# Quarter sums and weight sums on VectorE alone, a weight sum kept in DRAM, rope keys rotated in place, and query latents split earlier, in a one-core mixer kernel

## The chip, the cores and the metric

The kernel runs on one core of a Trainium2 chip. The metric is device time in microseconds of one execution. The kernel before was timed three times: 641.77, 641.38 and 640.35 us, with a median of 641.38 us. A profiled execution of it took 643.46 us, and the span from its first to its last instruction is 641.7 us.

## The reference

One inference step of a diffusion trunk with one layer: 128 prompt tokens and 1024 latent tokens (9 blocks of 128 rows), width 1024. Cut to what matters:

```python
h = rmsnorm(x) * (1 + scale) + shift              # scale, shift, gate from conditioning
u, v, g_a, c_q, c_kv, k_rope, g_b = split(h @ w_in)   # 512,512,512,256,128,64,512 columns
# group A: gated MLP over positions, 4 heads x 128, chunks of 128 positions
v = rmsnorm(gelu(v)) * g_v
a = gelu(u) * (einsum('hpq,bnqhd->bnphd', w_s, v) + b_s) * silu(g_a)
# group B: latent attention, 4 heads, low-rank queries and keys
q = rmsnorm(c_q) @ w_uq;  ckv = rmsnorm(c_kv);  k_rope = rope(k_rope)
attn = softmax(q_nope @ k_nope + rope(q_rope) @ k_rope) @ v     # latents also read 256 cached keys
y = x + gate * (concat(a, attn * silu(g_b)) @ w_o)
return rmsnorm(y) (prompt, latents), ckv, k_rope
```

## The kernel before, in words

**Numbers in two parts.** Every fp32 product is made of rounded parts: a value is rounded to a high part, the rest is a low part, and TensorE makes high x high, high x low and low x high. So each operand costs two evictions: a rounding ("high", on ScalarE or GpSimd) and a subtraction ("low", `lo_of`, L126, on VectorE alone).

**The seven products.** The columns u, g_a and g_b (1536, in three groups `q` = 0, 1, 2, each of two column blocks `j`) of the input projection are computed for the 1024 latent tokens by a scheme that needs seven products of half size where eight are usual. Their names are phases 1, 2, 5, 6, 3, 7, 4; "b" is a helper for the prompt. `SEQ` (L773) lists them in the order of work: 1 and 2 for all q, then 5 and 6, then "b" and 3, then 7 and 4. The matmuls are L868 (`pr`), 24 for one phase and column block in four groups of chunks, into a pool of six PSUM banks (`psa`). The prompt's products (L1006, `pps`) run between them and take a bank of a second pool of two (`pst`).

The activations come in four quarters A11, A12, A21, A22 (tiles `area00` to `area11`, high and low part of each). Phases 1, 2 and 4 read quarters as they are. Phases 5, 6, 7 and 3 read *quarter sums* s1, s2, s3, s4 (`sum_steps`, L957). For each half g of the rows: s1 is three additions (`s1a`, `s1b`, `s1c`), and s2, s3 and s4 are two each, from one another: s1 = A21 + A22, s2 = s1 - A11, s3 = A22 - s2, s4 = A12 - s2. One addition is a 128x1024 fp32 instruction (L968) on whichever of VectorE and GpSimd is to be done first. s1 lies in `mixB`, s2 and later s4 in `ss`, s3 in `st`. Each sum is then split (steps `ah`, `a`) over the quarter that it replaces as moving operand.

The weights come by DMA as raw tiles of 512 KB (`wr`, L786) on SP's queue. Phases 5, 6, 7 and 4 need *weight sums* (`weight_steps`, L792): `ws5` (L803), `ws6` (L812), `ws7` (L820), and for phase 4 two, `wt4` (L829) and `ws4` (L833). Then come the high part (`wh`) and the low part (`w`, L126) of the weights, in tiles `wop`. Raw tiles and `wop` pairs are few (`raw`: 2, later 3; `wop`: 2, later 3), so a load waits until an earlier raw tile is split.

**Around them.** Up to about 130 us the kernel modulates and transposes x and makes v and the gate: after GELU (L605) and statistics, `divide` (L619) scales v by its norm, most blocks on GpSimd, and TensorE mixes positions (L624, `mixp`), which VectorE takes out into `mixA` (L628). From 160 us the norms of the latents follow (`stat_steps`), which also multiply the key latents in place in `zraw`. Late in the products the query latents are transposed (`cq_steps`, L1157: transposes into a `pst` bank, high part on ScalarE, low part on VectorE), the query weights are folded (`fold_steps`, L1094, from four loads `fr`), and the rope keys are rotated (`ropek_steps`, L1285 to L1295: two products in tiles `ka` and `kb`, added twice into `kd`, on VectorE or GpSimd). The keys are transposed (L1318, `kT`) and the queries made (`qn`, `qr`, and their transposes L1236 with evictions L1268 and L1269), and then the scores begin (L1499). Attention takes from about 336 to 540 us and the output projection the rest; the change leaves both as they are.

**What sets the order.** All steps from the gate stage to the keys are given to class `Plan` (L43) with an engine ("V" VectorE, "G" GpSimd, "S" ScalarE, "T" TensorE, "D" SP's loads, "X" bookkeeping; "vG" and "SG" a choice of two), a cost, the steps that it depends on, a priority and resources that it takes and gives. `run` is a list scheduler: at each moment it emits the ready step with the smallest priority. A step on VectorE ("v") that overlaps one on GpSimd is charged a longer cost. The order in which steps are emitted is the order of each engine's instructions, and each engine works in that order.

Of the kernel before, what the change touches and what calls it, by code (L numbers as in the profile page):

```python
# [18 lines left out]
P = 128  # L19
# [23 lines left out]
class Plan:  # L43
# [8 lines left out]
    def run(self):  # L52
# [4 lines left out]
        while left:  # L57
# [4 lines left out]
            for s in left:  # L62
# [46 lines left out]
def tile_hymba_step(ctx: ExitStack, tc: tile.TileContext, I, O):  # L109
# [442 lines left out]
    VG2, COST2, HIGH2 = "vG", (1.25, 2.2), (1.05, 1.3)  # L552
# [45 lines left out]
    def post_steps(ts_):  # L598
# [176 lines left out]
    NEEDS = {1: ((0, 0),), 2: ((1, 0),), 5: ((0, 0), (0, 1)), 6: ((1, 1),), "b": ((0, 1),), 3: ((1, 1),), 7: ((1, 1), (0, 1)), 4: ((0, 0), (1, 0))}  # L775
# [6 lines left out]

    def raw_load(ph, q, y, c, prio):
        def fn():
            raws[ph, q, y, c] = place_for((ph, q, y, c), f"wr{ph}{q}{y}{c}", [2, 4, P])
            nc.sync.dma_start(raws[ph, q, y, c], I["w_t"][4 * q + c : 4 * q + c + 3 : 2, :, 4 * y : 4 * y + 4, :].rearrange("j p k m -> p j k m"))  # L786

        before = [order["load"] + "!"] if order["load"] else [f"wq{NK - 1}"]
        order["load"] = f"wr{ph}{q}{y}{c}"
        load_step(order["load"], fn, before, prio, 1.7, takes=("raw", "large"))  # L790

    def weight_steps(ph, q, prio):  # L792

        for y, c in NEEDS[ph]:
            raw_load(ph, q, y, c, prio)
        keys = [(ph, q, y, c) for y, c in NEEDS[ph]]
# [3 lines left out]
        if ph == 5:  # L800

            def total(e):
# [6 lines left out]
        elif ph == 6:  # L809

            def total(e):
# [4 lines left out]
            loaded = [f"ws6{q}"]  # L816
        elif ph == 7:

            def total(e):
# [5 lines left out]
            src, loaded, gone = (lambda: tsum[7, q]), [f"ws7{q}"], []  # L825
        elif ph == 4:

            def first(e):
                e.tensor_tensor(r(0), r(0), tsum[7, q], op=ALU.add)  # L829
                leave((7, q, 1, 1))  # L830

            def total(e):
# [3 lines left out]
            step(f"wt4{q}", VG2, COST2, first, [loaded[0], f"ws7{q}", f"w7{q}"], prio, gives=("raw", "large"))  # L836
            step(f"ws4{q}", VG2, COST2, total, [loaded[1], f"wt4{q}"], prio, gives=("raw", "large"))
# [434 lines left out]

    kd = {}

    def ropek_steps(t0, n):

        cell = {}

# [735 lines left out]
```

## Time and profile before

| | |
|---|---|
| median of three runs | 641.38 us |
| the profiled execution | 643.46 us |
| its span | 641.7 us |
| mean granted TensorE clock | 0.974 |
| TensorE busy | 612.9 us (96% of the span) |
| VectorE busy | 416.7 us (65%) |
| ScalarE busy | 286.2 us (45%) |
| GpSimd busy | 160.5 us (25%) |
| chain that ended last | PE 85%, DVE 6%, ACT 3%, issue 2%, DMA 1%, POOL 1% |

PE is TensorE's matmuls, PEld its weight loads, DVE VectorE, ACT ScalarE, POOL GpSimd, SP the engine that issues most DMAs. A row of the timeline gives start and length in us, engine, line, operation, the tile written, an arrow, and the tiles read, shapes, a count, and in brackets the idle time of the engine ahead of it with what ended it. A row of the groups gives busy time and mean ns of one. A row of the waits gives the total, how often, and the longest.

### The profile page before, as it was taken

How to read it: one execution, taken by the hardware profiler on the slowest of the kernel's cores; microseconds unless marked ns; L12 is line 12 of the kernel's file. 1: busy time of each engine (PE TensorE's matmuls, PEld its weight loads, DVE VectorE, ACT ScalarE, POOL GpSimd, SP SyncE). 2: the span in 40 equal slices, each digit the busy share in tenths (PEclk: the TensorE clock that was granted, in tenths of full speed). 3: DMA queues.
4: the chain of work that ended last, by engine and by line, in shares of the span. 5: the costliest groups of instructions: out<-in, count | busy, mean ns of one | idle time of the engine just before them, and what ended most of it. 6: DMA issues, size and time to landing. Idle time of an engine off the chain costs nothing.

```text
span 641.7 us, 9495 instructions
## 1 busy us (share of the span) xinstructions
PE 612.9 (96%) x3567; PEld 524.3 (82%) x3567; DVE 416.7 (65%) x838; ACT 286.2 (45%) x627; POOL 160.5 (25%) x145
## 2 busy tenths in 40 slices
PE   7799989999997999999789999999999999999995
PEld 6577877888885878888778899999999989888884
DVE  4435576714649875899685666577677666396655
ACT  4455864314242233444664555555555643232222
POOL 3523143102017220235352222123233241000001
PEclk8799989999999899999899999999999999999998
DMA  8970504401322424660100000000100112523211
GB/s 323 355 275 24 162 1 166 133 33 39 100 98 91 136 95 133 194 206 25 50 2 0 2 1 1 2 1 2 30 4 34 34 66 99 196 100 132 96 69 65
DMA packets 24509, 57.31 MB, mean 89 GB/s; under 512 B 2304, under 2 KB 6800, under 8 KB 24464
## 3 DMA queue, kind: packets, MB, share of 16 engines
q1 hardware_dynamic: 24320, 56.52, 25.7%
q8 instruction: 28, 0.46, 0.3%
q10 hardware_dynamic: 144, 0.20, 0.1%
q14 instruction: 17, 0.14, 0.1%
HBM read 51.88 MB, written 4.83 MB: 88 GB/s over the span
## 4 chain that ended last, share of the span: by engine, by line
PE 85%; DVE 6%; ACT 3%; issue 2%; DMA 1%; POOL 1%; SPq 0%; ACTq 0%; POOLq 0%
PE pr L868 16%; PE pT L1542 5%; PE w L1792 5%; PE w L1791 5%; PE w L1793 5%; PE s L1499 3%; PE o L1566 3%; PE o L1568 3%; PE o L1567 3%; PE s L1500 3%; PE s L1501 3%; PE s L1503 3%; PE s L1502 3%; PE vacc L402 3%; PE pps L1006 2%
## 5 line engine op out<-in xcount | busy, mean ns | idle before, releaser
L868 PE MATMUL pr<-area,wop 128*128 128x512 f32 x504 | 128.9, 398 | 4.7 <-DVE wop L126 2.9
L868 PEld LDWEIGHTS pr<-area,wop 128*128 128x128 f32 x504 | 91.7, 191 | 22.8 <-DVE wop L126 4.2
L126 DVE TENSOR_TENSOR pl<-pT,ph 128x512 fp32r<-128x512 f32 x81 | 55.4, 686 | 45.6 <-ACT ph L1546 45.3
L1490 POOL TENSOR_SCALAR e<-e,rs 128x1280 f32<-128x1280 f32 x32 | 42.8, 1338 | 138.7 <-DVE rs L1489 117.7
L1484 ACT ACTIVATE e<-s,nb,scl 128x256 f32<-128x256 f32 x64 | 56.1, 881 | 39.4 <-DVE nb L1478 33.3
L1546 ACT CAST ph<-pT 128x512 fp32r<-128x512 f32 x80 | 45.5, 590 | 40.0 <-PE pT L1542 37.2
L1791 PE MATMUL w<-area,areap 128*128 128x512 f32 (+1 forms) x152 | 57.8, 381 | 0.0
L1793 PE MATMUL w<-area,ml 128*128 128x512 f32 (+1 forms) x152 | 57.5, 378 | 0.0
L1792 PE MATMUL w<-area,areap 128*128 128x512 f32 (+1 forms) x152 | 57.5, 378 | 0.0
L1542 PE MATMUL pT<-ident,e 128*128 128x128 f32 x320 | 47.9, 273 | 0.7 <-DVE pl L126 0.7
L1566 PE MATMUL o<-ph,vh 128*128 128x256 f32 x160 | 48.1, 300 | 0.0
L1568 PE MATMUL o<-ph,vl 128*128 128x256 f32 x160 | 45.0, 281 | 0.0
L1567 PE MATMUL o<-pl,vh 128*128 128x256 f32 x160 | 44.9, 281 | 0.0
L1542 PEld LDWEIGHTS pT<-ident,e 128*128 128x128 f32 x320 | 37.8, 140 | 4.3 <-DVE pl L126 1.5
L1474 DVE TENSOR_REDUCE m<-s 128x1 f32<-128x1024 f32 x32 | 38.9, 1216 | 3.1 <-PE s L1503 3.1
L1499 PE MATMUL s<-kch,area 128*128 128x512 f32 (+1 forms) x96 | 38.5, 401 | 1.3 <-DVE areap L126 1.3
L126 DVE TENSOR_TENSOR wop<-wr,wop 128x1024 fp32r<-128x1024 f32 x21 | 32.6, 1553 | 9.9 <-ACT wop L557 6.3
L126 DVE TENSOR_TENSOR area<-hf,area 128x256 fp32r<-128x256 f32 (+3 forms) x25 | 17.2, 693 | 26.7 <-ACT hf L394 26.6
L1500 PE MATMUL s<-kcl,area 128*128 128x512 f32 (+1 forms) x96 | 34.6, 360 | 0.0
L1501 PE MATMUL s<-kch,area 128*128 128x512 f32 (+1 forms) x96 | 34.4, 359 | 0.0
L1503 PE MATMUL s<-krl,area 128*128 128x512 f32 (+1 forms) x96 | 34.3, 357 | 0.0
L1502 PE MATMUL s<-krh,area 128*128 128x512 f32 (+1 forms) x96 | 34.3, 357 | 0.0
(352 smaller groups left out, 1431.1 us busy)
## 6 DMA issues: line engine op xcount, KB each, us to landing
wr<-in_w_t SPq DMA_DIRECT2D x30, 512.0 KB, 3.7
ada<-in_ada_ss SPq DMA_DIRECT2D x16, 512.0 KB, 9.6
xr<-in_x SPq DMA_DIRECT2D x9, 512.0 KB, 3.9
adag<-in_ada_g SPq DMA_DIRECT2D x8, 512.0 KB, 3.3
wor<-in_w_o SPq DMA_DIRECT2D x8, 512.0 KB, 3.7
out_y<-y SPq DMA_DIRECT2D x8, 512.0 KB, 2.7
x<-in_x SPq DMA_DIRECT2D x6, 512.0 KB, 5.9
wvr<-in_w_v SPq DMA_DIRECT2D x8, 256.0 KB, 7.0
```

Source lines behind the costliest of these rows:

```text
L126: V.tensor_tensor(lo, src, f32(hi), op=ALU.subtract)
L868: T.matmul(ps, w[a][:, j % 2, k, :], x[:, k, b, :], start=first and ph in FIRST, stop=last, skip_group_check=ph not in FIRST)
L1484: S.activation(e[:, sl], src, AF.Exp, bias=nb, scale=scl[:, t : t + 1], accum_out=su[:, i : i + 1])
L1499: T.matmul(ps, qh_, kch[:, sl], start=True, stop=False)
L1500: T.matmul(ps, qh_, kcl[:, sl], start=False, stop=False)
L1542: T.transpose(ps[:, w : w + P], es[t, h][:, c * P : (c + 1) * P], ident)
L1566: T.matmul(o, vh[:, kt, :], ph[:, sl], start=c == 0, stop=False)
L1567: T.matmul(o, vh[:, kt, :], pl[:, sl], start=False, stop=False)
L1568: T.matmul(o, vl[:, kt, :], ph[:, sl], start=False, stop=c == n - 1)
L1791: T.matmul(ps, a, woh[k][:, c0:c1], start=k == 0, stop=False)
L1792: T.matmul(ps, a, wol[k][:, c0:c1], start=False, stop=False)
L1793: T.matmul(ps, b, woh[k][:, c0:c1], start=False, stop=k == NK - 1)
```

## The change

It does five things.

1. **One engine for the sums.** `VG2` becomes "v": all quarter sums and weight sums go to VectorE. The divides `gv` all go to VectorE too. The charge for an overlap of VectorE and GpSimd in `Plan.run` is computed from speeds of 0.36 and 0.67.
2. **A weight sum kept.** The sum `ws6` of phase 6 is also, up to rounding, the first sum of phase 4. A step `wt6` writes it to a DRAM tile `t2d` (three times 512 KB, on SP's queue), and phase 4 loads it (`wr4qt`) in place of the raw tile of weights that it took before; `wt4` is gone. The raw tile of phase 6 is given back only after the write has landed and phase 6's low part is made. The raw tile of phase 7 is given back after its low part.
3. **s4 in s1's place.** s4 is built in `mixB` where s1 was, and no longer in `ss`. So s3 waits only for `openB` (the end of the stage before) and s4 for the split of s1, and neither for the split of s2. For the last two column blocks `w5r` waits for the split of s4.
4. **Rope keys in place.** The rotation goes to VectorE, writes back into `zraw`, and reads tables of its own (`rk`, two more loads of 256 KB); it waits for its latents' statistics no longer, only for the projection. The doubling into `kd` becomes one copy on ScalarE.
5. **Query latents sooner.** The pool `zp` of the split query latents is opened in `open2` (when phases 6's and 7's sums are split and s4 is made) and not in `open3`; `cq` steps depend on `open2`.

The core of the diff:

```diff
@@ Plan.run
-                    r = min(self.shares[other] - now, 2 * cost)
-                    mine, theirs = (0.5 * r, 0.3 * r) if eng == "v" else (0.3 * r, 0.5 * r)
-                    cost += mine
+                    r = self.shares[other] - now
+                    slow, fast = (0.36, 0.67) if eng == "v" else (0.67, 0.36)
+                    if cost / slow <= r / fast:
+                        cost = cost / slow
+                        theirs = (1 - fast) * cost
+                    else:
+                        cost += (1 - slow) * r / fast
+                        theirs = r / fast - r
...
-    VG2, COST2, HIGH2 = "vG", (1.25, 2.2), (1.05, 1.3)
+    VG2, COST2, HIGH2 = "v", 1.25, (1.05, 1.3)
@@ post_steps
-            if j == 1 and n == 3:
-                step(f"gv{t}", "V", 0.72, lambda t=t, j=j: divide(j, t, V), [f"rv{t0}"], 0.5)
-            else:
-                step(f"gv{t}", "G", 1.1, lambda t=t, j=j: divide(j, t, G), [f"rv{t0}"], 1)
+            step(f"gv{t}", "v", 0.72, lambda t=t, j=j: divide(j, t, V), [f"rv{t0}"], 0.5)
@@ NEEDS, raw_load, weight_steps (NEEDS of phase 4: ((0, 0), (1, 0)) becomes ("t", (1, 0)))
+    t2d = gd.tile([3, P, 1024], F32, tag="t2d", name="t2d")
+            if y == "t":
+                raws[ph, q, y, c] = place_for((ph, q, y, c), f"wr{ph}{q}t", [2, 4, P])
+                nc.sync.dma_start(raws[ph, q, y, c], t2d[q].rearrange("p (j k m) -> p j k m", j=2, k=4))
+                return
...
-            loaded = [f"ws6{q}"]
+            loaded, gone = [f"ws6{q}"], []
+            step(f"wt6{q}", "D", 1.7, lambda: nc.sync.dma_start(t2d[q].rearrange("p (j k m) -> p j k m", j=2, k=4), r(0)), [f"ws6{q}"], prio - 0.5, lag=2.2)
+            step(f"wu6{q}", "X", 0.0, lambda: leave(keys[0]), [f"wt6{q}", f"w6{q}"], 0, gives=("raw", "large"))
...
-            def first(e):
-                e.tensor_tensor(r(0), r(0), tsum[7, q], op=ALU.add)
-                leave((7, q, 1, 1))
...
-            step(f"wt4{q}", VG2, COST2, first, [loaded[0], f"ws7{q}", f"w7{q}"], prio, gives=("raw", "large"))
-            step(f"ws4{q}", VG2, COST2, total, [loaded[1], f"wt4{q}"], prio, gives=("raw", "large"))
+            step(f"ws4{q}", VG2, COST2, total, loaded, prio, gives=("raw", "large"))
@@ sum_steps
-            sum_step(f"s3a{g}", lambda made=made: made(st, "st"), lambda q=q: q(A22, 0), lambda q=q: q(A22, 1), add, [f"a6.{g}"], 3.2)
+            sum_step(f"s3a{g}", lambda made=made: made(st, "st"), lambda q=q: q(A22, 0), lambda q=q: q(A22, 1), add, ["openB"], 3.2)
-            sum_step(f"s4a{g}", lambda here=here: here(ss), lambda q=q: q(A12, 0), lambda here=here: here(ss), sub, [f"a6.{g}", f"s3b{g}"], 3.1)
+            sum_step(f"s4a{g}", s1, lambda q=q: q(A12, 0), lambda here=here: here(ss), sub, [f"a5.{g}", f"s2b{g}"], 3.1)
@@ cq_steps, ropek_steps, open2
-        step(f"cp{t0}", "T", 0.22 * n, pe, ["open3"], 2.6 + 0.01 * t0, takes=("pst",))
+        step(f"cp{t0}", "T", 0.22 * n, pe, ["open2"], 2.6 + 0.01 * t0, takes=("pst",))
...
+            V.tensor_tensor(kr(0, 64), kr(0, 64), rk[0][:, ts_, :], op=ALU.mult)
+            V.tensor_tensor(kr(0, 64), kr(0, 64), cell["b"], op=ALU.add)
...
+            S.copy(kd[t0], kr(0, 64).unsqueeze(2).broadcast_to([P, n, 2, 64]))
...
-        step("open2", "X", 0.0, open2, [f"a{ph}.{g}" for ph in (7, 3) for g in range(2)], 0)
+        step("open2", "X", 0.0, open2, [*(f"a{ph}.{g}" for ph in (6, 7) for g in range(2)), "s4a0", "s4a1"], 0)
```

Lines of the changed kernel are 5 to 12 higher than before at these places (L968 becomes L975, L126 becomes L131, L619 becomes L624, L868 becomes L875).

GpSimd, at the first divides of the gate stage (L619, after whose `gv` TensorE mixes) and the first quarter sums (L968 into `mixB`), before:

```order
L129 TENSOR_SCALAR wq2_746<-wqr3_723 128x448
L619 TENSOR_TENSOR gv0_706<-gv0_706,vv3r_835 128x512
L619 TENSOR_TENSOR gv2_740<-gv2_740,vv3r_835 128x512
L968 TENSOR_TENSOR mixB_681<-mixB_681,area11_115 128x1024
L129 TENSOR_SCALAR wq4_997<-wqr4_730 128x448
L968 TENSOR_TENSOR mixB_681<-mixB_681,area11_115 128x1024
```

VectorE at the same place now (`areap` and `area11` are low parts of the transposed x):

```order
L131 TENSOR_TENSOR area11_115<-hf240_880,area11_115 128x256
L624 TENSOR_TENSOR gv0_707<-gv0_707,vv3r_835 128x512
L624 TENSOR_TENSOR gv1_714<-gv1_714,vv3r_835 128x512
L131 TENSOR_TENSOR areap_116<-hf241_902,areap_116 128x128
L624 TENSOR_TENSOR gv2_741<-gv2_741,vv3r_835 128x512
L131 TENSOR_TENSOR area11_115<-hf250_894,area11_115 128x256
L131 TENSOR_TENSOR areap_116<-hf251_918,areap_116 128x128
```

The divides have gone from GpSimd to VectorE, three within five instructions, and no quarter sum stands among them on either engine.

VectorE from the weight sum of phase 5 (`wr5001`, L803) on, where phases 2 and 5 meet; `wop122` is the low part of the weights for the last third of phase 2, `wop150` and `wop160` those for phases 5 and 6, before:

```order
L803 TENSOR_TENSOR wr5001_1754<-wr5001_1754,wr5000_1713 128x1024
L126 TENSOR_TENSOR wop122_1794<-wr2210_1637,wop022_1793 128x1024
L1027 TENSOR_TENSOR mixA_94<-mixA_94,poT10_1802 128x2x128
L126 TENSOR_TENSOR area00_112<-ss0_1552,area00_112 128x2x512
L968 TENSOR_TENSOR st0_1839<-area11_115 128x1024
L126 TENSOR_TENSOR area00_112<-ss1_1554,area00_112 128x2x512
L126 TENSOR_TENSOR wop150_1848<-wr5001_1754,wop050_1847 128x1024
L968 TENSOR_TENSOR ss0_1552<-area01_113,ss0_1552 128x1024
L812 TENSOR_TENSOR wr6011_1800<-wr6011_1800,wr5001_1754 128x1024
L968 TENSOR_TENSOR ss0_1552<-ss0_1552,area01_113 128x1024
L126 TENSOR_TENSOR wop160_1906<-wr6011_1800,wop060_1905 128x1024
```

Now, with the rotation's last two instructions (L1307, L1308) ahead:

```order
L1307 TENSOR_TENSOR zraw_685<-zraw_685,rk0_1560 128x4x64
L1308 TENSOR_TENSOR zraw_685<-zraw_685,kb4_1762 128x4x64
L813 TENSOR_TENSOR wr5001_1751<-wr5001_1751,wr5000_1702 128x1024
L131 TENSOR_TENSOR wop122_1793<-wr2210_1627,wop022_1792 128x1024
L1034 TENSOR_TENSOR mixA_94<-mixA_94,poT10_1800 128x2x128
L131 TENSOR_TENSOR area00_112<-ss0_1564,area00_112 128x2x512
L141 TENSOR_SCALAR zzt_1760<-zv_1756 128x18
L131 TENSOR_TENSOR area00_112<-ss1_1580,area00_112 128x2x512
L131 TENSOR_TENSOR wop150_1846<-wr5001_1751,wop050_1845 128x1024
L142 TENSOR_SCALAR zzr_1759<-zzt_1760 128x18
L143 TENSOR_SCALAR zzw_1761<-zv_1756 128x18
L822 TENSOR_TENSOR wr6011_1815<-wr6011_1815,wr5001_1751 128x1024
```

The quarter sums are gone from between the splits; all twelve of s2, s3 and s4 stand ahead of this piece, and the small steps of the latents' statistics (`zz`) have come into it. On GpSimd five large sums (four of L968, one of L812) that ran at the same time are gone.

TensorE at the second fold (L1094, now L1101), before in the seventh product:

```order
L868 MATMUL pr73_2444<-area11_115,wop041_2462 128x512 x2
L868 MATMUL pr73_2444<-area11_115,wop141_2463 128x512
L1094 MATMUL fold1_2557<-fr2_2494 128x128 x2
L1094 MATMUL fold1_2557<-fr3_2514 128x128 x2
L868 MATMUL pr73_2444<-area11_115,wop041_2462 128x512 x2
```

Now:

```order
L1101 MATMUL fold0_2601<-fr0_2153 128x128 x2
L1101 MATMUL fold0_2601<-fr1_2580 128x128 x2
...
L1330 MATMUL kT41_2635<-ident_75,kd4_2151 128x128 x4
L1101 MATMUL fold1_2640<-fr2_2609 128x128 x2
L1101 MATMUL fold1_2640<-fr3_2614 128x128 x2
L875 MATMUL pr74_2576<-area11_115,wop042_2606 128x512 x2
L875 MATMUL pr74_2576<-area11_115,wop142_2607 128x512
```

Both folds and the first key transposes now stand in the last product, the second fold ahead of its last 24 matmuls; the transposes of the query latents (`cqT`), which were around the folds, stand in the third product.

More of the change, by code (lines that the diff above doesn't have):

```diff
@@ L1273, in tile_hymba_step, with ropek_setup, tables @@
     kd = {}
+    rk = {}
+    def ropek_setup():
+        def tables():
+            for i in range(2):
+                rk[i] = place_for(("rk", i), f"rk{i}", [NS, 64])
+                nc.sync.dma_start(rk[i], I["rope"][:, i])
+        load_step("rk", tables, ["openB"], 1.5, 1.0, takes=("slot", "slot"))
+        step("rkx", "X", 0.0, lambda: leave(("rk", 0), ("rk", 1)), ["kr0", "kr4"], 0, gives=("slot", "slot"))
     def ropek_steps(t0, n):
         cell = {}
+        ts_ = slice(t0, t0 + n)
```

76 lines of the change are left out of this document (35 added, 41 removed).

## The prediction

> **What bounds the kernel now.** I read the head of the page first, then the list of TensorE's waits, then the time slices, and last the timelines around the waits.
>
> ```profile
> span 641.7 us, 9495 instructions
> PE 612.9 (96%) x3567; PEld 524.3 (82%) x3567; DVE 416.7 (65%) x838; ACT 286.2 (45%) x627; POOL 160.5 (25%) x145
> ```
>
> TensorE is busy for 612.9 of 641.7 us, and the change takes no matmul away. So it can only win what is in the other 28.8 us, and what TensorE does at a lower clock. The list of TensorE's waits (total, times, longest) says who is late:
>
> ```profile
> PE qrT L1236 <- DVE area L1269: 3.2, 2, 2.4
> PE pr L868 <- DVE wop L126: 2.9, 3, 1.7
> PE mixp L624 <- POOL mixB L968: 2.0, 1, 2.0
> PE pr L868 <- ACT wop L557: 1.5, 1, 1.5
> PE s L1499 <- DVE areap L126: 1.3, 1, 1.3
> ```
>
> The second, third and fourth stand where the change moves work; the first and last are the passage from the products to attention. The slices (after the bounds: the length, then busy time of PE, PEld, DVE, ACT, POOL, then granted clock, DMA share, GB/s) show how a short wait grows:
>
> ```profile
> 90.00:100.00 10.00, 10.00 (x54) 8.49 (x55) 6.89 (x18) 5.98 (x29) 4.35 (x4) 0.83 0.15 48
> 150.00:190.00 40.00, 40.00 (x208) 34.50 (x207) 23.52 (x42) 13.21 (x25) 5.92 (x5) 1.00 0.30 95
> 200.00:210.00 10.00, 7.95 (x37) 5.95 (x36) 9.97 (x6) 2.75 (x4) 5.14 (x2) 0.98 0.32 107
> 210.00:220.00 10.00, 10.00 (x39) 8.12 (x38) 9.97 (x9) 3.15 (x3) 3.25 (x1) 0.85 0.32 103
> ```
>
> From 150 to 190 TensorE is full and VectorE idle for 16.5 of 40 us; from 200 to 220 VectorE is full and TensorE waits, then runs at a granted clock of 0.85. A clock of 0.83 over 10 us is 3.4 us at half speed, which costs 1.7 us of matmuls.
>
> **The gate stage, 82 to 94 us (A).**
>
> ```profile
> 82.57 2.22 POOL L619 TENSOR_TENSOR gv<-gv,vv3r 128x512 f32<-128x512 f32 x2 [11.73 <-ACT area L393]
> 86.68 2.43 POOL L968 TENSOR_TENSOR mixB<-mixB,area 128x1024 f32<-128x1024 f32 x1 [1.89 <-ACT area L393]
> 86.80 2.93 DVE L126 TENSOR_TENSOR area<-hf,area 128x256 fp32r<-128x256 f32 x2
> 89.99 3.65 PE L624 MATMUL mixp<-wsT,gv 128*128 128x128 f32 x16 [2.00 <-POOL mixB L968]
> 108.02 1.05 PE L624 MATMUL mixp<-wsT,gv 128*128 128x128 f32 x8
> 183.69 0.69 DVE L892 TENSOR_TENSOR mixA<-mixA,c 128x512 f32<-128x512 f32 x1 [1.04 <-ACT c L919]
> ```
>
> TensorE waits 2.00 us, by the profile's inference until GpSimd's quarter sum L968 is out, then takes 3.65 us for 16 matmuls. Eight take 1.05 elsewhere, so 16 should take about 2.0, or 2.1 as two rows of eight; I book 1.55. After the change VectorE does the divides gv0 to gv2 and the quarter sum is gone from both engines there. The statistics are ready when the divide starts at 82.57; with three divides at 0.69 (the row of the same shape) and two or three short splits between, the third ends near 85.7, and the matmuls would otherwise run on from about 88.0 (89.99 less 2.00), so 2.3 us are to spare. A: **-3.55** (bounds -2.0 and -3.7).
>
> **The shared stretch, 190 to 236 us (B, C, D).**
>
> ```profile
> 190.73 1.22 DVE L968 TENSOR_TENSOR st<-area 128x1024 f32<-128x1024 f32 x1
> 191.82 4.26 PE L868 MATMUL pr<-area,wop 128*128 128x512 f32 x18
> 192.83 2.40 POOL L968 TENSOR_TENSOR st<-st,ss 128x1024 f32<-128x1024 f32 x1
> 192.90 3.41 DVE L126 TENSOR_TENSOR area<-ss,area 128x1024 fp32r<-128x1024 f32 x1 [0.95 <-POOL area L129]
> 195.19 3.37 POOL L968 TENSOR_TENSOR st<-area 128x1024 f32<-128x1024 f32 x1
> 199.56 3.40 DVE L968 TENSOR_TENSOR ss<-area,ss 128x1024 f32<-128x1024 f32 x1
> 199.69 0.50 PE L868 MATMUL pr<-area,wop 128*128 128x512 f32 x1 [1.74 <-DVE wop L126]
> 202.88 3.42 DVE L812 TENSOR_TENSOR wr<-wr,wr 128x1024 f32<-128x1024 f32 x1
> 207.49 0.73 PE L868 MATMUL pr<-area,wop 128*128 128x512 f32 x2 [1.52 <-ACT wop L557]
> 208.75 23.66 PE L868 MATMUL pr<-area,wop 128*128 128x512 f32 x96 [0.53 <-DVE wop L126]
> 233.08 3.25 PE L868 MATMUL pr<-area,wop 128*128 128x512 f32 x13 [0.67 <-DVE wop L126]
> ```
>
> A VectorE instruction of this size takes 1.22 us alone and 3.4 us beside GpSimd's sums, which take 2.4 to 3.4. In 13.3 us (192.9 to 206.2) four VectorE and four GpSimd instructions get through; all eight on VectorE alone would take 8 x 1.22 = 9.8.
>
> The waits there are 1.74, 1.52, 0.53 and 0.67. After the third, 96 matmuls take 23.66. At 4.26 for 18 they would take 22.7 at most (96/18 x 4.26) and 22.0 if the end of the last one is counted once (0.228 from start to start), so the half clock cost 1.0 to 1.7; the clock of 0.85 in 210 to 220 and 0.98 in 200 to 210 gives (0.15 + 0.02) x 10 = 1.7, which I take.
>
> What must hold is that VectorE has its new work done in time.
>
> ```profile
> 155.05 3.28 DVE L126 TENSOR_TENSOR wop<-wr,wop 128x1024 fp32r<-128x1024 f32 x1 [3.40 <-PE zacc L719]
> L1295 DVE TENSOR_TENSOR kd<-ka,kb x4: 417/420/422, 300.8 to 301.8; 128x256 f32<-128x256 f32 x4
> L812 DVE TENSOR_TENSOR wr<-wr,wr 128x1024 f32<-128x1024 f32 x2 | 4.6, 2318 | 0.0
> L829 DVE TENSOR_TENSOR wr<-wr,wr 128x1024 f32<-128x1024 f32 x3 | 5.8, 1929 | 0.0
> ```
>
> The eight sums s3 and s4 and one of s2 come into 150 to 190: 9 x 1.22 = 11.0. The key rotation comes too: per four blocks two rows of 128x256 at 0.42 and two of half that, 1.25, and 2.5 for both. Less goes: the 3.28 at 155.05 falls to 1.23. So 11.0 + 2.5 - 2.05 = 11.5 of the 16.5 us free, and 5 stay. In VectorE's new order the split `wop122`, which phase 2's last third needs, stands behind all this and behind the output adds that wait for TensorE up to about 184.4. I make it done near 188.0, against 190.8 when TensorE takes it up: 2.8 us to spare, the tightest place. From 190 to 213, with the sums gone and nothing on GpSimd but single roundings, VectorE has about 11 us of work where it had 22, and by my walk through its queue every later split comes 3 to 8 us early. B, C and D: -(1.74 + 1.52 + 0.53 + 0.67) - 1.7 = **-6.2** (bounds -4.5, if the clock falls anyway, and -6.2).
>
> **The sixth product's sum in DRAM.** Three sums of L829 (5.8 us on VectorE, mean 1929 ns) go from 270 to 300 us, with the key rotation's tail there; TensorE is dense in that stretch, so this is worth nothing. Added are three writes on SP's queue, each ahead of a weight load, and a buffer held longer.
>
> ```profile
> out_y<-y SPq DMA_DIRECT2D x8, 512.0 KB, 2.7
> fr<-in_w_qk SPq DMA_DIRECT2D x4, 192.0 KB, 4.0
> ```
>
> No row has a write in this place; the nearest, a write of the same size, lands after 2.7. SP waits for the sum before it issues, and the load of the next pair's weights queues behind. The DMA engines are busy to a third there (share 0.32 in the rows of 200 to 220), and I estimate 4 to 6 us to spare: 0. From above it costs 3 x 2.7 = 8.1 if no write is covered. It gains nothing below 0, because the number of reads stays the same. The reads of it come some 40 us later and replace loads of equal size. The two loads of rope tables at the front are off every tight place: 0.
>
> **Earlier query latents, later fold.** The transposes of the latents go from the seventh product to the third, into a two-bank pool that the prompt's products share.
>
> ```profile
> L1161 ACT CAST cqh<-cqT x5: 372/577/588, 282.0 to 294.6; 128x512 fp32r<-128x512 f32 x4, 128x256 fp32r<-128x256 f32 x1
> L126 DVE TENSOR_TENSOR cql<-cqT,cqh x5: 413/678/683, 283.2 to 295.1; 128x512 fp32r<-128x512 f32 x4, 128x256 fp32r<-128x256 f32 x1
> ```
>
> A bank is held for about 0.58 + 0.68 behind its transposes. In TensorE's new order a prompt product follows three matmuls (0.7 us) after the last two of them and wants such a bank: +0.5 (0 to 1.3). The second fold now stands right ahead of the last 24 matmuls, and three of the four `fr` loads come behind the last weight load: at most one landing, 4.0; I take +0.9. The fourth product's matmuls wait for VectorE's adds of the seventh, and the key transposes now hold banks of the products through the last of them: +0.4 (0 to 1.0). **+1.8** in all.
>
> **The passage to attention (F).**
>
> ```profile
> 299.75 4.49 PE L868 MATMUL pr<-area,wop 128*128 128x512 f32 x19
> 304.08 1.03 PE L1318 MATMUL kT<-ident,kd 128*128 128x128 f32 x8
> 315.48 0.66 PE L1236 MATMUL qrT<-ident,r 128*128 128x128 f32 x2 [2.43 <-DVE area L1269]
> 335.87 0.80 PE L1499 MATMUL s<-kch,area 128*128 128x512 f32 x1 [1.34 <-DVE areap L126]
> ```
>
> The last product ends at 304.24 and the scores begin at 335.87. These 31.6 us are set by VectorE's evictions, with three waits of TensorE. In the new order 12 query matmuls (12 x 0.237 = 2.8) that stood ahead of the last product come behind it, and 8 key transposes (1.03) go ahead. The stretch is not TensorE's, so it takes the 2.8 mostly for nothing; ahead of it 1.8 are saved, and I give back 0.3 for a longer stretch: **-1.5** (-3.5 to +1.5, where a further half-clock stretch of 1.7 would come in).
>
> **Sum.** -3.55 - 6.2 + 1.8 - 1.5 = **-9.45**. The profiled execution took 643.46 (span 641.7), 2.1 above the median of 641.38; its stalls are those of the kernel's order, so I take the sum off the median: 641.38 - 9.45 = **631.9 us**.
>
> **The rivals.** (1) *The waits come back elsewhere.* The cover of 2.8 us at `wop122` is thin, and two of the new waits may fall into one clock window and cost 1.7 more, or F keeps its length. A stays won, of B to D and F half: -3.55 - 3.1 - 0.75 + 1.8 = -5.6, **636**. For it: in 190 to 213 three waits follow one another on a full VectorE, and one of 2.00 or 1.52 + 0.53 was followed by half clock, one of 1.74 was not. Against: the 16.5 us idle. 0.22. The Trainium skill ("TensorE: Matmul & The Clock Gate", Part 1) gives the clock gate a free-running window of 3413 ns, by which waits of 0.5, 0.9 and 0.4 cost nothing more apart and 1.7 more only where they meet in one window; the waits just named agree.
>
> (2) *More goes than I count.* New waits at 0 and F at -3.5: -3.55 - 6.2 - 3.5 = -13.25, **628**. 0.13.
>
> (3) *The writes to DRAM are late loads.* Of the 8.1 us three quarters show, the rest as forecast: -9.45 + 6.1 = -3.4, **638**. For it: SP issues in order and the write waits for a sum. Against: the spare 4 to 6 us. 0.07.
>
> (4) *VectorE becomes the bound: slower.* All quarter sums stand in its one queue between 155 and 190. At 1.22 each, 5 us stay free. It turns if the 12 sums s2 to s4 there cost more than 1.22 + (5 + 9.45)/12 = 2.4 us. Two groups of the same shape did: 1929 and 2318 ns on average, 3.4 at worst. Halfway from 2.3 to 3.4 it is 12 x 1.64 - 5 = 14.7 late, plus a half-clock stretch of 1.7, less 9.45: +6.9, **648**. Against: those means hold instructions slowed by GpSimd, and its sums are what goes. 0.05. The Trainium skill ("Perfetto Trace Analysis", Optimizing Scalar/DVE Operations) advises moving work off a saturated VectorE to another engine, the reverse of this change, and adds that GpSimd might not help since the two share a read port; by its first half the order of before would be the faster one, by its second this change, and the rows of 192 to 206 agree with the second.
>
> (5) *No change*: the waits are not VectorE's and GpSimd's sharing but the order's, and come back one for one at the next tight places: 641.38 + 0, **641**. For it: the profile only infers who released a wait. Against: the rows of 192.8 to 206, where the same instruction takes 1.22 or 3.4 by its neighbour. 0.03.
>
> **How the numbers follow.** The forecast, 631.9, has 0.50; its likely terms (F from -3.5 to +1.5, the new waits from 0 to 3) reach from 628 to 636. The range takes in rivals (1) and (2) and most of (3): **627 to 638.5**. About 0.2% (1.3 us) is what a measurement of this kernel can tell from no change. Faster: 0.50 + 0.22 + 0.13 + 0.07 = **0.92**; same **0.03**; slower **0.05**.
>
> **What would show it.** Right: no wait and full clock at the mixing matmuls before 100 us; no quarter sum on GpSimd, and VectorE's at 1.2 us each; no wait of the products on a split or sum from 190 to 236, with clock 1.00 there; new waits under 2 us before the folds; scores beginning about 31 us after the last product. Wrong: a wait at the first matmuls that use `wop122`; a weight load that lands behind a write to DRAM; a half-clock stretch in 235 to 305 us, where there was none; a passage to attention that is 3 us longer.

## The result and the profile after

The changed kernel took 633.0 us (632.89 to 634.77, four runs) beside 641.07 us of the kernel before (640.35 to 641.77, four runs): a ratio of 0.9881 with a 95% interval of 0.9860 to 0.9902. That is 8.1 us less by the medians (7.65 by the means, on which the ratio rests), where the forecast had 9.45 less; 633.0 lies in its range.

The head of the page after:

```profile
span 631.1 us, 9486 instructions
PE 607.2 (96%) x3567; PEld 519.6 (82%) x3567; DVE 409.0 (65%) x853; ACT 288.7 (46%) x631; POOL 121.3 (19%) x122
```

Between the two profiled executions the span fell by 10.6 us, more than the medians. Of that 5.7 us are TensorE's busy time at the same number of matmuls: seven stretches at half clock before, four after. Part of the difference has nothing to do with the change. The same matmul of the modulation stage, ahead of all that was edited, starts at these times in the profiles of before and after:

```profile
37.19 0.50 PE L374 MATMUL mod<-sel,rows 128*128 128x2 f32 x4
```

```profile
35.59 0.50 PE L379 MATMUL mod<-sel,rows 128*128 128x2 f32 x4
```

So 1.6 us of the 10.6 were there before the kernels differ. In the fourteen profiles of this study that matmul starts anywhere from 34.96 to 37.36 us. Spans of single executions are therefore compared here from a common landmark, and the totals by medians.

TensorE's list of waits after (the larger ones from the gate stage to the scores):

```profile
PE qrT L1243 <- DVE area L1276: 2.1, 2, 1.3
...
PE gps L750 <- DMA adag<-in_ada_g: 1.8, 2, 1.3
...
PE qr L177 <- DVE area L1276: 1.0, 1, 1.0
...
PE s L1513 <- DVE areap L1276: 0.6, 1, 0.6
...
PE poT L1027 <- ACT po L1022: 0.5, 1, 0.5
...
PE pps L1013 <- DVE cql L131: 0.5, 1, 0.5
...
PE pr L875 <- DVE w L949: 0.2, 1, 0.2
```

The waits of the mixing matmuls (2.0) and of the products on splits (2.9 and 1.5) are gone. New are 1.8 on the gate loads, where there were 0.3, two of 0.5 behind the earlier latents, and 1.0 at the queries (`qr`). The slices of the stages that the prediction spoke of:

```profile
90.00:100.00 10.00, 10.00 (x62) 7.33 (x61) 6.45 (x24) 3.05 (x17) 1.70 (x3) 1.00 0.31 105
150.00:190.00 40.00, 40.00 (x208) 34.24 (x207) 32.22 (x38) 14.87 (x27) 4.19 (x3) 1.00 0.28 92
200.00:210.00 10.00, 10.00 (x46) 8.29 (x45) 8.13 (x17) 1.05 (x1) 0.00 (x0) 1.00 0.60 209
210.00:220.00 10.00, 10.00 (x46) 8.29 (x45) 8.22 (x14) 2.89 (x3) 0.00 (x0) 1.00 0.48 168
```

TensorE is full in each and the clock is 1.00. VectorE went from 23.5 to 32.2 us in 150 to 190, and from full to four fifths in 200 to 220. The gate stage and the tight place of the products, and the groups of the quarter sums (after the bar: busy time and mean ns of one):

```profile
80.63 1.29 DVE L624 TENSOR_TENSOR gv<-gv,vv3r 128x512 f32<-128x512 f32 x2
...
82.23 0.68 DVE L624 TENSOR_TENSOR gv<-gv,vv3r 128x512 f32<-128x512 f32 x1
...
86.27 1.95 PE L629 MATMUL mixp<-wsT,gv 128*128 128x128 f32 x16
...
182.63 1.22 DVE L131 TENSOR_TENSOR wop<-wr,wop 128x1024 fp32r<-128x1024 f32 x1
...
186.96 0.86 PE L875 MATMUL pr<-area,wop 128*128 128x512 f32 x3
```

```profile
L975 DVE TENSOR_TENSOR mixB<-mixB,area 128x1024 f32<-128x1024 f32 x6 | 7.3, 1215 | 0.0
...
L975 DVE TENSOR_TENSOR mixB<-area,ss 128x1024 f32<-128x1024 f32 x2 | 3.3, 1639 | 0.0
```

The divides end at 82.9, and the 16 matmuls take 1.95 us without a wait. The split at 182.63 is `wop122`. It is done at 183.85, and the group of matmuls that first needs it starts at 186.96: 3.1 us to spare, where the prediction had worked out 2.8. The sums take 1.2 us each, but for the pair with one instruction beside a GpSimd rounding.

The passage to attention and its waits:

```profile
286.78 5.72 PE L875 MATMUL pr<-area,wop 128*128 128x512 f32 x24
...
304.32 0.41 PE L1243 MATMUL qrT<-ident,r 128*128 128x128 f32 x2 [0.86 <-DVE area L1276]
...
306.25 0.64 PE L1243 MATMUL qrT<-ident,r 128*128 128x128 f32 x2 [1.29 <-DVE area L1276]
...
325.48 0.50 PE L1513 MATMUL s<-kch,area 128*128 128x512 f32 x1
```

From the last product (292.50) to the first score it is now 33.0 us, where it was 31.6, with the 2.8 us of query matmuls inside that used to stand ahead of the last product.

### The profile page after: what moved, and what is told of

Its sections match the earlier page's. It is cut to its first block, busy times and chain, and to the rows that moved or that the text cites. A ratio compares the mean times of both kernels' runs of the same rounds, so it can differ in the third digit from the quotient of the medians.

```text
span 631.1 us, 9486 instructions
## 1 busy us (share of the span) xinstructions
PE 607.2 (96%) x3567; PEld 519.6 (82%) x3567; DVE 409.0 (65%) x853; ACT 288.7 (46%) x631; POOL 121.3 (19%) x122
## 4 chain that ended last, share of the span: by engine, by line
PE 87%; DVE 4%; ACT 3%; DMA 3%; issue 2%; POOL 0%; SPq 0%; ACTq 0%; DVEq 0%
PE pr L875 18%; PE pT L1556 5%; PE w L1806 5%; PE w L1805 5%; PE w L1807 5%; PE o L1580 3%; PE o L1582 3%; PE o L1581 3%; PE vacc L407 3%; PE s L1513 3%; PE s L1515 3%; PE s L1514 3%; PE s L1517 3%; PE s L1516 3%; PE vacc L409 2%; PE vacc L408 2%
## 5 line engine op out<-in xcount | busy, mean ns | idle before, releaser
L875 PE MATMUL pr<-area,wop 128*128 128x512 f32 x504 | 123.9, 393 | 0.2 <-DVE w L949 0.2
L875 PEld LDWEIGHTS pr<-area,wop 128*128 128x128 f32 x504 | 91.7, 188 | 17.2 <-issue 0.6
L131 DVE TENSOR_TENSOR pl<-pT,ph 128x512 fp32r<-128x512 f32 x81 | 55.4, 686 | 46.2 <-ACT ph L1560 46.0
L131 DVE TENSOR_TENSOR wop<-wr,wop 128x1024 fp32r<-128x1024 f32 x21 | 26.7, 1271 | 10.8 <-PE zacc L721 6.1
L1807 PEld LDWEIGHTS w<-area,ml 128*128 128x128 f32 x152 | 28.6, 188 | 5.4
```

The source lines that it names most:

```text
L131: V.tensor_tensor(lo, src, f32(hi), op=ALU.subtract)
L875: T.matmul(ps, w[a][:, j % 2, k, :], x[:, k, b, :], start=first and ph in FIRST, stop=last, skip_group_check=ph not in FIRST)
L1807: T.matmul(ps, b, woh[k][:, c0:c1], start=False, stop=k == NK - 1)
```

## The experiments

Theory: the gain comes from no longer letting VectorE and GpSimd run sums side by side. Rival: it comes from the new order (s3 and s4 made early, latents early, the sum in DRAM), and the engine of the sums matters little. Each kernel was timed beside the kernel before on the same chip, and the ratio is to that.

**Sums on either engine again.** In the changed kernel:

```diff
-    VG2, COST2, HIGH2 = "v", 1.25, (1.05, 1.3)
+    VG2, COST2, HIGH2 = "vG", (1.25, 2.2), (1.05, 1.3)
```

> The changed kernel, with the quarter sums and weight sums again on whichever of VectorE and GpSimd is to be done first (divides stay on VectorE, and all the rest of the change stays). If the gain of the products came from ending the sharing, sums beside one another cost 2.4 to 3.4 us again, waits on splits come back behind 160 us, and most of the 6.2 us go: 637 to 640 us. If it came from the other parts (looser waits of s3 and s4, earlier latents, the sum kept in DRAM), the time stays at 633 to 634.

Measured: 641.9 us, ratio 1.0013 (0.9995 to 1.0030). All of the gain is gone, more than was expected. Its timeline:

```profile
99.76 5.22 POOL L975 TENSOR_TENSOR mixB<-mixB,area 128x1024 f32<-128x1024 f32 x2
...
100.16 2.36 DVE L142 TENSOR_SCALAR vv3r<-vv3t 128x12 int32<-128x12 int32 x1
...
102.56 0.17 DVE L149 TENSOR_TENSOR vv3t<-vv3r 128x12 f32<-128x12 f32 x1
...
102.77 2.24 DVE L150 TENSOR_TENSOR vv3t<-vv3t,vv3w 128x12 f32<-128x12 f32 x1
...
107.31 1.13 PE L629 MATMUL mixp<-wsT,gv 128*128 128x128 f32 x8 [3.15 <-DVE gv L624]
...
193.36 6.91 PE L875 MATMUL pr<-area,wop 128*128 128x512 f32 x22 [2.42 <-DVE wop L131]
```

The planner put two of s1's additions on GpSimd at 99.76, beside the statistics of the gate. Statistics of 128x12 elements take 0.17 us alone; the two that meet those additions take 2.36 and 2.24, about as long as a GpSimd sum. The chain of statistics is late, and TensorE waits 3.15 at the mixing matmuls. The wait of 2.42 on a split is back too, with half clock behind it (granted 0.83 in 190 to 200). So the other parts of the change together, without the engine, are worth nothing that this measurement can tell. In this run and the next the planner orders every engine anew, so each shows the engine together with the order that goes with it; the idle sums below keep the order.

**Sums and divides on VectorE only, in the kernel before.** The reverse test, one part alone:

```diff
-    VG2, COST2, HIGH2 = "vG", (1.25, 2.2), (1.05, 1.3)
+    VG2, COST2, HIGH2 = "v", 1.25, (1.05, 1.3)
...
+            step(f"gv{t}", "v", 0.72, lambda t=t, j=j: divide(j, t, V), [f"rv{t0}"], 0.5)
```

> The kernel before with one part of the change alone: quarter sums, weight sums and divides on VectorE only (the charge for an overlap plays no part then; s3 and s4 stay late). If ending the sharing is most of the gain: the gate stage wins its 3.5 us and the products half of theirs, 635 to 637. If all parts are needed together: 639 to 641.

Measured: 630.16 us, ratio 0.9823 (0.9798 to 0.9848): faster than expected, and faster than the whole change (0.9860 to 0.9902). Its slices where the kernel before waited:

```profile
190.00:200.00 10.00, 10.00 (x52) 8.44 (x51) 10.00 (x9) 2.89 (x5) 1.89 (x1) 1.00 0.39 107
200.00:210.00 10.00, 10.00 (x46) 8.29 (x45) 9.76 (x12) 2.11 (x2) 0.00 (x0) 1.00 0.45 139
```

VectorE is as full there as before, with s3 and s4 still late, and TensorE does not wait: a sum or split there now takes 1.2 us, but for one of 2.06 beside a rounding on GpSimd. With the kernels before and after this makes a square: sums on either engine, the rest old 641 and the rest new 641.9; sums on VectorE, the rest old 630.2 and the rest new 633.0. The engine is worth 9 to 11 us in both rows. The rest costs about 2.8 once the sums are on VectorE. The square is not quite clean: the divides move with the sums where the rest is old and stay on VectorE where it is new (the run with the divides below finds 0.2 us for them), and the planner's charge for an overlap differs.

**Idle sums on GpSimd.** The changed kernel, with GpSimd additions of a tile that nobody reads. The first version had six, three emitted behind the step s4a1 and three behind wh22, ordered only by GpSimd's queue:

```diff
+            G.tensor_tensor(scr[0], scr[0], scr[0], op=ALU.add)
```

> The changed kernel with six idle GpSimd sums of 128x1024 (of a tile that nobody reads) beside VectorE's queue from 160 to 187 us; every other engine's order is the same. If sharing slows VectorE, each takes about 2.2 us from VectorE (3.4 in place of 1.22): 13 us in its queue, of which some 3 are idle time and 3 are spare at the split of the last weights of phase 2; TensorE then waits about 7 there and loses 1.7 more to half clock: 640 to 643. If the order is what counts: 633 to 634.

Measured: 633.08 us, ratio 0.9866 (0.9837 to 0.9894): a miss.

```profile
129.68 9.80 POOL L1437 TENSOR_TENSOR spare<-spare 128x1024 f32<-128x1024 f32 x3
...
178.21 6.61 POOL L1437 TENSOR_TENSOR spare<-spare 128x1024 f32<-128x1024 f32 x3
...
178.44 1.93 DVE L1064 TENSOR_SCALAR zv<-ssz 128x9 f32<-128x9 f32 x2
...
187.21 1.22 DVE L131 TENSOR_TENSOR wop<-wr,wop 128x1024 fp32r<-128x1024 f32 x1
...
188.45 0.86 PE L875 MATMUL pr<-area,wop 128*128 128x512 f32 x3
```

Three of the six had nothing to wait for and ran at 129.68, beside nothing that mattered. The other three ran from 178 to 185, and `wop122` is done at 188.43, 4.6 later than in the changed kernel, of which 1.5 is where this execution stood in the early stages. The 3.1 us that were spare at that split are used up: the group starts at 188.45, and only because its third matmul, at 188.92, is the first to read `wop122` are 0.5 left. The run shows the size of the cover rather than a price. The second version has eight, two behind s2b0, three behind wh21 and three behind wh22, which read a tile of s2 and so start when it is made:

```diff
+            G.tensor_tensor(scr[0], ss[0], ss[0], op=ALU.add)
```

> The changed kernel with eight idle GpSimd sums that read a tile of s2, so that they run from about 158 to 187 us beside VectorE's queue; the orders of all other engines are the same. In the run with six, three of them fell into that stretch and made the last split of phase 2's weights 3.1 us later, just what was spare there. If sharing is the price, eight take some 17 us from VectorE, 3 of them idle and 3 spare: a wait of about 10 us and half clock, 641 to 647. If VectorE's order alone counts: 633 to 634.

Measured: 640.91 us, ratio 0.9991 (0.9974 to 1.0007).

```profile
165.21 7.99 POOL L1435 TENSOR_TENSOR spare<-ss 128x1024 f32<-128x1024 f32 x3
...
166.24 2.91 DVE L975 TENSOR_TENSOR st<-area 128x1024 f32<-128x1024 f32 x1
...
169.07 4.68 DVE L899 TENSOR_TENSOR mixA<-mixA,c 128x512 f32<-128x512 f32 x2
...
176.07 0.80 PE L875 MATMUL pr<-area,wop 128*128 128x512 f32 x1 [3.44 <-DVE wop L131]
...
193.73 0.50 PE L875 MATMUL pr<-area,wop 128*128 128x512 f32 x1 [1.86 <-DVE wop L131]
```

TensorE's, VectorE's and ScalarE's orders are those of the changed kernel, and 7.9 us of its 8.1 are gone. A sum of VectorE takes 2.91 in place of 1.22, and two waits on splits come to 5.3 us, besides half clock. The price per idle sum was nearer 1.7 than the 2.2 that was expected, which puts the time just under the expected range. The mechanism is shown: work on GpSimd that nothing needs makes the kernel slower by what VectorE loses beside it.

**Divides on GpSimd again**, in the changed kernel:

```diff
-            step(f"gv{t}", "v", 0.72, lambda t=t, j=j: divide(j, t, V), [f"rv{t0}"], 0.5)
+                step(f"gv{t}", "G", 1.1, lambda t=t, j=j: divide(j, t, G), [f"rv{t0}"], 1)
```

> The changed kernel, with the divides of the gate stage on GpSimd again (all but one of the first three), and no quarter sum there. If the first wait came from the quarter sums on both engines, two divides at 1.1 us alone are ready in time and the time stays within 0.7 of the changed kernel: 632.5 to 634. If the divides on GpSimd are late by themselves, the wait of 2 us and its half clock come back: 635 to 637.

Measured: 633.16 us, ratio 0.9869 (0.9844 to 0.9893), as the first theory had it.

```profile
80.00:90.00 10.00, 10.00 (x59) 8.41 (x58) 5.93 (x18) 8.79 (x26) 2.28 (x3) 1.00 0.01 2
```

TensorE does not wait in 80 to 90 with the divides on GpSimd. The first wait of the kernel before came from the quarter sums on both engines, not from the divides.

**s3 and s4 late**, in the changed kernel, with the same order on TensorE:

```diff
-            sum_step(f"s3a{g}", lambda made=made: made(st, "st"), lambda q=q: q(A22, 0), lambda q=q: q(A22, 1), add, ["openB"], 3.2)
+            sum_step(f"s3a{g}", lambda made=made: made(st, "st"), lambda q=q: q(A22, 0), lambda q=q: q(A22, 1), add, [f"a6.{g}"], 3.2)
-            sum_step(f"s4a{g}", s1, lambda q=q: q(A12, 0), lambda here=here: here(ss), sub, [f"a5.{g}", f"s2b{g}"], 3.1)
+            sum_step(f"s4a{g}", s1, lambda q=q: q(A12, 0), lambda here=here: here(ss), sub, [f"a6.{g}", f"a5.{g}", f"s3b{g}"], 3.1)
```

> The changed kernel, with s3 and s4 made only after the split of s2, as before, but all on VectorE; TensorE's order is the same. If sharing is what cost, eight sums at 1.22 us (9.8 us) fit into the 11 us that VectorE has free from 190 to 213, and the time stays at 633 to 634.5. If making s3 and s4 early is what won, the waits on the splits of phases 5 and 6 come back: 636 to 639.

Measured: 638.75 us, ratio 0.9952 (0.9926 to 0.9978; single runs from 635.12 to 640.15).

```profile
219.99 10.07 PE L875 MATMUL pr<-area,wop 128*128 128x512 f32 x43 [2.04 <-DVE wop L131]
```

Here the rival has a share: in the changed kernel early sums are worth 5.8 us by the medians (4.6 by the ratios), although VectorE's sums cost 1.2 either way. In the kernel before with the sums on VectorE the same late sums made no wait. So the early sums make good what other parts of the change took at that place. The traces point to the writes to DRAM. With the sums late, SP's second write stands in its queue from 201 until the sum that it writes is made at 209.07. A load of phase 5's last weights stands behind it: what that load waits for itself was done at 206.01, yet it goes out at 209.53 and lands at 213.98. In the kernel before with the sums on VectorE, which has no writes, the same load goes out at 206.16 and lands at 209.75; in the changed kernel, where the sum comes early, it goes out at 205.43. The weight sum that reads it starts at 214.80 in place of 209.85, and its split is the one that TensorE waits for at 219.99. No run has the late sums without the writes, so that the writes are the whole cost, and the rotation of the keys and the statistics have no part in it, is not shown.

**Latents late**, in the changed kernel:

```diff
-        step(f"cp{t0}", "T", 0.22 * n, pe, ["open2"], 2.6 + 0.01 * t0, takes=("pst",))
+        step(f"cp{t0}", "T", 0.22 * n, pe, ["open3"], 2.6 + 0.01 * t0, takes=("pst",))
```

> The changed kernel with the query latents transposed as late as before (after the first blocks' results). If the earlier split takes nothing off TensorE's path, as the forecast had it (a wait of 0.5 on a bank is its only trace): 632.5 to 633.5. If it frees VectorE where the last products and the queries need it: 634.5 to 636.

Measured: 629.86 us, ratio 0.9816 (0.9789 to 0.9843): 3.1 us less than the changed kernel, outside both expectations. The waits of 0.5 and 0.5 on the banks and on the prompt's output are gone, and at the start of the passage the clock does not fall. The slice 300 to 310 with the latents early and, below it, late:

```profile
300.00:310.00 10.00, 7.43 (x39) 5.73 (x37) 7.89 (x13) 5.97 (x11) 2.13 (x3) 0.83 0.01 2
```

```profile
300.00:310.00 10.00, 8.70 (x44) 6.69 (x45) 8.10 (x13) 6.32 (x12) 5.03 (x6) 1.00 0.00 1
```

With the latents early TensorE waits 0.86 and 1.29 close together and runs 3.4 us at half clock (1.7 us); with them late no wait in 300 to 310 is over 0.6. The profiles of all seven kernels here that have the change's early latents show half clock behind the two waits at this place, and none of the four with late latents does. So 1.0 + 1.7 of the 3.1 us are seen in the profile. That GpSimd takes more of the queries' rotation in the second (5.03 us of busy time against 2.13) goes with it; it was not tried by itself.

**Without the sum in DRAM**, in the changed kernel, and then also with the latents late:

```diff
-            step(f"wt6{q}", "D", 1.7, lambda: nc.sync.dma_start(t2d[q].rearrange("p (j k m) -> p j k m", j=2, k=4), r(0)), [f"ws6{q}"], prio - 0.5, lag=2.2)
...
+            step(f"wt4{q}", VG2, COST2, first, [loaded[0], f"ws7{q}", f"w7{q}"], prio, gives=("raw", "large"))
```

> The changed kernel without the weight sum in DRAM: phase 4 loads its raw tile again and makes two sums on VectorE, three of 1.22 us more, and SP has three writes fewer. By the forecast the three sums lie under a dense TensorE and the writes cost nothing: 632.5 to 634. If VectorE's load in 245 to 290 us matters, or the shorter hold of raw tiles: 635 to 638; if the writes held up loads: 631 to 632.

> The changed kernel with the latents late and without the sum in DRAM. If the sum in DRAM is worth 2 to 3 us by itself, as leaving it out of the changed kernel cost: 632 to 633. If it only makes room on VectorE for the early latents: 629.5 to 630.5, as with the late latents alone.

Measured: 635.77 us, ratio 0.9898 (0.9864 to 0.9932), and with the latents late 631.64 us, ratio 0.9852 (0.9828 to 0.9875). By the medians the sum in DRAM is worth 2.8 and 1.8 us, but each pair of intervals overlaps. In the profile the first has a wait of 1.0 us on a split that the changed kernel has not:

```profile
PE pr L878 <- DVE wop L131: 1.0, 1, 1.0
...
PE pps L1016 <- DVE cql L131: 0.8, 1, 0.8
```

The first time is in the second of the expectations of its run, the second time lies between those of its own. So the part probably gains 1 to 3 us where the forecast had nothing, its size not settled. Whether the gain lies in the three sums on VectorE or in the raw tiles, which are given back at other times, was not tried.

**Late latents and late sums**, to see whether the cost of the late sums hangs on the early latents:

> The changed kernel with the latents late and s3 and s4 made late. The kernel before with sums on VectorE only had s3 and s4 late and no wait in the products. If late sums are harmless by themselves: 629.5 to 630.5. If the wait of 2.0 and 0.3 us that the late sums made in the changed kernel comes from the load that the rest of the change puts on VectorE there (rotation, later statistics): 632 to 635.

Measured: 633.80 us, ratio 0.9887 (0.9866 to 0.9908). That is 3.9 more than with late latents alone, and the wait of 2.0 on a split is there again: it does not hang on the latents. SP's second write again holds the load of phase 5's last weights, which goes out at 209.51.

**The gate loads.** The plan counts 2.2 us from the issue of such a load to its landing; the traces have 3.2. In the changed kernel with late latents, and in the kernel before with sums on VectorE, it was set to 3.6:

```diff
-            load_step(f"gl{j}.{i}", lambda i=i: load(i), [], 3 + 0.1 * j, 1.6, takes=("ga",))
+            step(f"gl{j}.{i}", "D", 1.6, lambda i=i: load(i), [], 3 + 0.1 * j, takes=("ga",), lag=3.6)
```

> The changed kernel with the query latents late and with 3.6 us in place of 2.2 as the planned time from the issue of a gate load to its landing, so that the gate's matmuls are put behind their loads. If the 1.3 and 0.5 us that TensorE waits there were the price of getting there sooner: 1 to 1.5 less than with the late latents alone (629.9), 628.4 to 629. If the loads are the limit of that stage and the wait only moves: 629.5 to 630.5.

> The kernel before with sums and divides on VectorE only, and the planned landing of the gate loads at 3.6 us. By the first theory of the gate loads, 1 to 1.4 less than the 630.2 without: 628.8 to 629.2. By the second: 629.5 to 631.

Measured: 629.07 us, ratio 0.9810 (0.9786 to 0.9833), and 630.77 us, ratio 0.9840 (0.9818 to 0.9862). The wait on the gate loads is gone from both profiles, but neither is told apart from its kernel without the edit (0.9816 and 0.9823), and the second has a new wait of 0.8 on a split. The first time lies between its two expectations, the second is in the range of the second theory. Undecided. With the latents late alone (629.86) and with this edit (629.07) the kernel beats both of the kernels that were compared.

## Why the prediction was right, and where it was off

**What bounds it.** Right: the waits of TensorE on VectorE and GpSimd, and half clock behind them. The matmuls did not change, and the time did.

**A, -3.55.** Right in size, and in what was to blame: no wait, 16 matmuls in 1.95 us, and with the divides back on GpSimd but no quarter sum beside them there is no wait either. The path was another than the prediction had. It took the divides to be what TensorE needed. But in the kernel before two divides were done on GpSimd at 84.79 (82.57 + 2.22) and the third, on VectorE, at 85.33, 4.7 us before the matmuls start:

```profile
83.81 1.52 DVE L619 TENSOR_TENSOR gv<-gv,vv3r 128x512 f32<-128x512 f32 x1
...
89.43 0.46 ACT L394 ACTIVATE hf<-h,at 128x128 f32<-128x128 f32 x1 [2.03 <-DVE area L126]
```

By the semaphores in the trace, TensorE's queue waits at the mixing matmuls from 84.97 to 89.93 and is released by this copy on ScalarE, which ends at 89.89; the quarter sum that the list of waits names had ended 0.9 earlier, at 89.11. ScalarE had stood idle for 2.03 before it, behind VectorE's two splits at 86.80, which took 2.93 beside that quarter sum (one split of this shape takes 0.42 alone, at 81.89). So the quarter sum held VectorE's splits, they held ScalarE, and ScalarE held TensorE; the move of the divides had no part in the gain that shows, as the run with the divides found.

What the step left out stands right behind it. TensorE reaches the gate's matmuls sooner than their loads land:

```profile
107.73 0.64 PE L750 MATMUL gps<-adag,csp 128*32 128x256 f32 x8 [1.29 <-DMA adag<-in_ada_g]
...
118.06 0.64 PE L750 MATMUL gps<-adag,csp 128*32 128x256 f32 x8 [0.52 <-DMA adag<-in_ada_g]
```

That is 1.8 where there were 0.3, so 1.5 of the 3.55 were given back in this execution. It is near the gap between the forecast's 9.45 and the 8.1 measured, but that it is the cause of the gap is not shown. The wait differs from one execution to the next (0.9 in the profile with late latents, whose order is the same up to there), and three kernels without it are no faster than their likes beyond the noise: 633.16 with the divides on GpSimd against 633.0, 629.07 against 629.86 and 630.77 against 630.16 with the planned landing at 3.6. The prediction followed the end of this stall to what is late next in VectorE's queue and not in SP's.

**B, C and D, -6.2.** Right: no wait of the products (`pr`) on a split or sum from 190 to 236 and the clock at 1.00. The cover at `wop122` was put at 2.8 and was 3.1. The idle sums confirm it from both sides: three used 3.1 without a loss of time, eight cost 7.9 us. One reason was put too widely. The prediction counted on the sums being both on VectorE and out of 190 to 213. The square of four kernels shows that the engine alone is enough: with s3 and s4 still late, the kernel before won 10 to 11 us. With the rest of the change in place it is not: there late sums cost 5.8 us.

**The sum in DRAM, 0.** In the changed kernel the writes cost nothing that shows (with the sums late they hold a load, as rival (3) had it), and the price was right too:

```profile
t2d<-wr SPq DMA_DIRECT2D x3, 512.0 KB, 2.6
```

What was off is the gain: it was put at nothing, and leaving the part out cost 1.8 to 2.8 us by the medians, with overlapping intervals.

**Earlier latents and later folds, +1.8.** The bank's wait was put at 0.5 and is 0.48:

```profile
235.32 0.51 PE L1013 MATMUL pps<-wop0b,areap 128*128 128x256 f32 x2 [0.48 <-DVE cql L131]
...
241.11 0.44 PE L1027 MATMUL poT<-ident,po 128*128 128x128 f32 x2 [0.51 <-ACT po L1022]
```

The folds did not wait (0.9 was booked), the wait on VectorE's adds is 0.2 (0.4 was booked), and the prompt's output waits 0.5 on ScalarE, which was not foreseen: 1.0 in all, since 0.2 on the adds was there before. The cost of this part lies elsewhere, in the passage, where 1.7 of the 3.1 us of the run with late latents are half clock.

**F, -1.5.** Near in size, with luck: -2.8 + 1.0 for the moved matmuls, +1.4 for the longer stretch, so -0.4 to the first score, and by the first transposes of attention's probabilities (355.6 before, 344.5 after, against 335.87 and 325.48 for the scores) another 0.7 less, since the half clock that stood at 335.8 before is gone. The sum had 0.3 for the longer stretch, which was 1.4, and nothing for that half clock, which made good most of the rest. The half clock at its start remained.

**The sum.** -3.55 + 1.5 - 6.2 + 1.0 - 1.1 = -8.35, against 8.1 by the medians and 9.0 between the two profiles from the common landmark on (10.6 - 1.6). That it came so near to -9.45 is in part luck: the gate loads (1.5) and the longer passage (1.1) were missed, and 0.8 less of waits behind latents and folds and 0.7 of half clock went the other way. Forecast and likeliest case were right, and the rivals (2) to (5) did not come. Of rival (1), one piece did, the half clock in the passage with the early latents. Rival (4), VectorE as the bound, did not: its sums took 1.2 us, not 2.4. But the eight idle sums put the kernel near that point, at 640.9, with VectorE's sums at 2.9 beside GpSimd's.

## What to carry to other kernels

Two engines that slow each other should be priced as a pair in a planner, and the pair compared with one engine alone: four and four instructions took 13.3 us side by side and would take 9.8 on VectorE at 1.22 each. When a stall is taken away, look at what stands next on every queue that feeds the waiting engine, the loads included, and check the engine that a list of waits names: one whose work ended 0.9 us before the wait did was not the one that ended it. A change in several parts should be timed part by part: here one part was worth 10 to 11 us, and the others, which were to help it, took about 2.8 back.

## What was not expected of the hardware

The slowing does not go by size. Statistics of 128x12 elements, 0.17 us alone, took 2.2 to 2.4 us beside a GpSimd sum of 128x1024, and 128x9 took 1.9 for two beside the idle sums: a small instruction seems to wait for the other engine's instruction to end. The one of 2.24 ended at 105.01 and the GpSimd sums beside it at 104.98. A rounding on GpSimd, 1.05 us alone, and a VectorE sum beside it took 1.96 and 2.06. The same code ahead of every edit stood up to 2.4 us apart from one execution to the next (34.96 and 37.36). Of that, 0.7 were there when the first loads landed and 1.1 by 28 us; the rest comes with a half-clock stretch from about 25 us, which is 6.8 us long in the later one and 3.4 in the other.

Nor does the length of a wait alone decide whether half clock follows. The wait of 2.43 at the query transposes was followed by 3.4 us at half clock in the kernel before and in the same kernel with the sums on VectorE and the planned landing at 3.6, but by none with the sums on VectorE alone. One of 3.15, in the run with the sums on either engine, was followed by none, and one of 2.00 in the kernel before by 3.4 us. So part of what a stall costs, 1.7 us each time, is a matter of when it falls.
